# Order of transposes and copies, and softmax times v over two query blocks, in a streaming encoder step

## The chip, the cores and the metric

The kernel runs on one core of a Trainium2 chip. The metric is the device time of one execution in microseconds (us). TensorE (PE in the profile) multiplies and transposes, VectorE (DVE) and ScalarE (ACT) work elementwise and read the accumulators in PSUM, GpSimd (POOL) and SyncE (SP) mostly start transfers. Each engine works through its own instructions in order and waits for the others on semaphores.

## The reference

One layer of an encoder is applied to 1024 prompt rows and 64 sample rows (1088 in all) of width 1024. What the change touches is the attention; the layer reads:

```
h = rms_norm(x)
glu_a, glu_b, q, k, v, gates = split(h @ w_in)
u = glu_a * sigmoid(glu_b)
c = silu(layer_norm(causal_dwconv(u, width 31))) @ w_conv_out
for each of 16 heads (64 wide), each frame over its own 64-row chunk and the 8 chunks before:
    pr = softmax(q k^T / 8 + rel_bias)
    a = pr @ v
x = x + (sigmoid(gates_c) * c + sigmoid(gates_a) * (a @ w_att_out)) @ w_out
x = x + (gelu(causal_dwconv(up, width 3)) * gate) @ w_ffn_down        # up, gate from rms_norm(x) @ w_ffn_up
x = x + sigmoid(rms_norm(x) @ w_ple_gate) * (p @ w_ple_proj)
y = rms_norm(x)
```

Outputs are y, the new key and value caches and the convolution states, all in float32.

## The kernel before, in words

Activations stand with features on the 128 partitions and rows along the free dimension. A product of float32 operands is done as three products of their high and low parts (`mm3`, lines 154 to 166): a value is split by ACT, which copies the high part, and by DVE, which subtracts it (`split_into`, `w_split`).

The first part of the kernel, up to about 1010 us, makes the input projection in 40 + 16 jobs of 128 output columns (`order_1a`: gate `gb` and value `ga` of the GLU, `q`, `k`, `v`, the branch gates `s`). A job has three groups of rows (384, 384, 320 columns), a group 24 products of the type of line 159 to 161. Everything else is put between them by `tick`, which is called twice per group: in the middle (after 12 products) and at its end, after `evac` has emptied the accumulator. Ticks alternate; in this part those in the middle are "even" and those at the end "odd".

A head pair (two heads, 128 features) has nine query blocks, `p` = 0 to 7 of 128 prompt rows with 1, 2, 3, 4, 5, 5, 5, 5 key blocks of 128, and `p` = 8 with the 64 sample rows. A block goes through five steps:

- `step_S`, in an even tick: scores on PE into the PSUM tile `s_ps` (line 485), then on DVE the bias is added and a row minimum taken (line 491), which writes `s` to SBUF.
- `step_E`, same tick: exp on ACT (line 501).
- `step_R`, in the next odd tick: reciprocal on DVE (575), and ACT scales `s` (526).
- `step_T`, in the odd tick after that: PE transposes `s` block by block into the PSUM tile `t_ps` (511), and ACT copies that to `pt` (514; 516 and 519 for the sample block). `t_ps` holds both heads, one in each half, and shares its only buffer (tag `st`) with `s_ps`.
- `step_PV`, in the next even tick, behind the scores of a later block: softmax times v on PE into `o_ps` (536), its split into `aT` by ACT and DVE (170, 171), and a store to `a_d` by POOL (540), which is read back in the next part of the kernel.

Between those, `bg_tick` takes background work from a list: the 31 taps of the depthwise convolution on DVE (329), and from about 800 us the layer norm behind it (388 to 421), whose affine (409) and tanh (415) run on ACT. `tick` sums up the PE time that it reckons for a tick (`spent`), and 0.46 of it is what background work may cost. The order is thus fixed when the program is built; no scheduler moves it.

Of the kernel before, what the change touches and what calls it, by code (L numbers as in the profile page):

```python
# [9 lines left out]
F32 = mybir.dt.float32  # L10
F32R = mybir.dt.float32r
# [5 lines left out]
P = 128  # L17
# [58 lines left out]
def encoder_step(ctx: ExitStack, tc: tile.TileContext, I, O):  # L76
    nc = tc.nc
    dma_in = nc.sync.dma_start
    dma_st = nc.gpsimd.dma_start
# [17 lines left out]
    a_d = dram.tile([KT, P, 2, T], F32, name="a_d")  # L97
# [70 lines left out]
    def split_into(dst, c0, n, src, scale=1.0):  # L168

        nc.scalar.activation(out=dst[:, 0, c0:c0 + n], in_=src, func=AF.Copy, scale=scale)  # L170
        nc.vector.scalar_tensor_tensor(out=dst[:, 1, c0:c0 + n], in0=src, scalar=scale,
                                       in1=dst[:, 0, c0:c0 + n].bitcast(F32), op0=ALU.mult, op1=ALU.subtract)
# [47 lines left out]
    with tc.manual_schedule():  # L220
# [53 lines left out]
        at = att.enter_context(tc.tile_pool(name="att", bufs=1))  # L274
# [34 lines left out]
        def bg_tick(budget, most):  # L309
            debt[0] = min(debt[0] + budget, 2.5)  # L310
            while bg and debt[0] > 0 and most > 0:
                cost, fn = bg.pop(0)
                fn()
                debt[0] -= cost
                most -= 1
# [28 lines left out]
        st = {}  # L344
# [113 lines left out]
        cur = {}  # L458
        pipe = []
        stages = {"e": [], "t": [], "pv": []}  # L460
# [37 lines left out]
        def step_E(st):  # L498
            m, n = st["m"], st["n"]
            for s, sm in zip(st["s"], st["sm"]):  # L500
                nc.scalar.activation(out=s[0:m, 0:n], in_=s[0:m, 0:n], func=AF.Exp, scale=-1.0, bias=sm[0:m, 0:1],  # L501
                                     accum_out=sm[0:m, 1:2])

        def step_T(st):
            m, n = st["m"], st["n"]
            ps = ps_st[0].tile([P, 2, 1024], F32, tag="st", name="t_ps")
            st["pt"] = []
            for h, s in enumerate(st["s"]):
                for b in range(st["nb"]):
                    w = min(P, n - b * P)  # L510
                    nc.tensor.transpose(ps[0:w, h, b * P:b * P + m], s[0:m, b * P:b * P + w], ident[0:m, 0:m])  # L511
                pt = at.tile([P, 640], F32, tag="pt", name="pt", bufs=2)
                if m == P:
                    nc.scalar.activation(out=pt[:, 0:n], in_=ps[:, h, 0:n], func=AF.Copy)  # L514
                else:
                    nc.scalar.activation(out=pt[:, 0:512].rearrange("p (b q) -> p b q", q=P)[:, :, 0:m],
                                         in_=ps[:, h, 0:512].rearrange("p (b q) -> p b q", q=P)[:, :, 0:m],
                                         func=AF.Copy)
                    nc.scalar.activation(out=pt[0:64, 512:512 + m], in_=ps[0:64, h, 512:512 + m], func=AF.Copy)
                st["pt"].append(pt)  # L520

        def step_R(st):

            m, n = st["m"], st["n"]
            for s, sm in zip(st["s"], st["sm"]):
                nc.scalar.activation(out=s[0:m, 0:n], in_=s[0:m, 0:n], func=AF.Copy, scale=sm[0:m, 2:3])

        def step_PV(st):

            c, m, n, nb = cur[st["i"]], st["m"], st["n"], st["nb"]  # L530
            o_ps = ps_o.tile([P, 512], F32, tag="o", name="o_ps")
            for b in range(nb):
                w = min(P, n - b * P)
                for h in range(2):
                    a = 64 * h
                    nc.tensor.matmul(o_ps[a:a + 64, 0:m], lhsT=c["v"][0:w, st["vb"] + b, a:a + 64],  # L536
                                     rhs=st["pt"][h][0:w, b * P:b * P + m], start=(b == 0), stop=(b == nb - 1))
            aT = at.tile([P, 2, P], F32R, tag="aT", name="aT")
            split_into(aT, 0, m, o_ps[:, 0:m])
            dma_st(out=a_d[st["i"]][:, :, st["q0"]:st["q0"] + m], in_=aT[:, :, 0:m].bitcast(F32))  # L540

        pe_bg = []

        def tick(base=1.95):


            spent = base
            odd = turn[0]
            turn[0] = 1 - odd
            new = done = flip = None  # L550
            if not odd:
                if pipe:
                    new = pipe.pop(0)
                    spent += 1.1
                if stages["pv"]:
                    done = stages["pv"].pop(0)
                    spent += 0.218 * done["nb"] + 0.2
            elif stages["t"]:
                flip = stages["t"].pop(0)
                spent += 0.214 * flip["nb"]  # L560
            if new is not None:
                step_S(new)
            bg_tick(RATIO * spent, 1)
            if done is not None:
                step_PV(done)
            if new is not None:
                step_E(new)
                stages["e"].append(new)
            if flip is not None:
                step_T(flip)  # L570
                stages["pv"].append(flip)
            if odd:
                for st in stages["e"]:
                    for sm in st["sm"]:
                        nc.vector.reciprocal(out=sm[0:st["m"], 2:3], in_=sm[0:st["m"], 1:2])
                    step_R(st)
                    stages["t"].append(st)
                stages["e"].clear()
            if pe_bg:
                if pe_bg[0][0] <= 0:  # L580
                    pe_bg.pop(0)[1]()
                else:
                    pe_bg[0][0] -= 1
            bg_tick(0.0, 9)
# [58 lines left out]
        def job_group(kind, i, g, hl):  # L643
            c0, n = GR[g]
            ps_full = pjp.tile([P, 512], F32, tag="pj", name="pj")
            mm3(ps_full[:, 0:n], hl, hT, c0, n, hook=tick)
            evac(kind, i, g, ps_full[:, 0:n])
            tick()

        def evac(kind, i, g, ps):  # L650
                c0, n = GR[g]
# [27 lines left out]
                elif kind == "q":  # L679
                    c = cur[i]  # L680
                    split_into(c["Q"], c0, n, ps, scale=-0.125)
                elif kind == "k":
                    c = cur[i]
# [1 line left out]
                    for o, w, d in segs(c0, n, 0, SEQ + PAST):  # L685
                        nc.scalar.activation(out=kt[:, 0, d:d + w], in_=ps[:, o:o + w], func=AF.Copy)
                    if g == 1:
                        c["kst"] = at.tile([P, 640], F32, tag="pt", name="kst", bufs=2)
                        nc.scalar.activation(out=c["kst"][:, 0:256], in_=ps[:, 128:384], func=AF.Copy)
                    elif g == 2:  # L690
                        nc.scalar.activation(out=c["kst"][:, 256:576], in_=ps, func=AF.Copy)
                        dma_st(out=O["k_new"][i], in_=c["kst"][:, 0:576])
# [3 lines left out]
                elif kind == "v":  # L696
                    c = cur[i]
# [174 lines left out]
        while pipe or stages["t"] or stages["pv"] or pe_bg or bg:  # L872
            tick()
# [597 lines left out]
        for ci, ch in enumerate(chunks[:-1]):  # L1471
# [23 lines left out]
            for f in range(f0, KT):  # L1495
                hl = w_use()
                for g, (c0, n) in enumerate(GR):
# [5 lines left out]
                    if g == 1 and f in nxt:  # L1503
                        pool, tag = (bp, "pb") if ci == 1 else (ap_, "pair")
# [145 lines left out]
```

## Time and profile before

| what | value |
|---|---|
| median of 3 runs | 2203.5 us (2201.48 to 2205.72) |
| profiled execution | 2199.4 us, its span 2197.3 us |
| PE busy | 2094.6 us, 95% of the span |
| DVE, ACT, POOL busy | 1320.1, 829.8, 224.2 us |
| mean granted clock of TensorE | 0.99 of full speed |

The profile is of one execution. "Busy" is the time in which an engine worked; "idle before" is the time for which it stood still ahead of an instruction, with the engine and line whose end released it. PE's matmuls overlap, so a run of them is best measured from start to start. PEld is TensorE's weight load, which overlaps PE.

### The profile page before, as it was taken

The page shows a single profiled execution, that of the slowest core. Times are in us where ns is not written, and L with a number is a line of the kernel's source. Part 1 is how long each engine was busy: PE and PEld are TensorE (multiplying, and loading weights), DVE is VectorE, ACT ScalarE, POOL GpSimd, SP SyncE. Part 2 cuts the span into 40 slices and gives each one's busy share as a digit, 9 for nine tenths or more (in the row PEclk, how much of TensorE's full clock was granted, in tenths as well). Part 3 has the DMA queues.
Part 4 walks back from the last instruction along what each step waited for, and adds up shares of the span by engine and source line. Part 5 has one row for each costly group of instructions (what it writes and reads, how often), then busy time and mean ns, then how long its engine had stood idle before and what let it go on. Part 6 is the DMA issues. An engine that isn't in the chain of part 4 may idle for free.

```text
span 2197.3 us, 35659 instructions
## 1 busy us (share of the span) xinstructions
PE 2094.6 (95%) x14696; PEld 2012.2 (92%) x14696; DVE 1320.1 (60%) x2246; ACT 829.8 (38%) x1583; POOL 224.2 (10%) x453
## 2 busy tenths in 40 slices
PE   8989899999999998979999999999999999999997
PEld 6979798988888887869999999999999999999997
DVE  6676676676766645343235457777777763345644
ACT  5352635344545446473012334333333331113421
POOL 4000101101010111111000000000000020000400
PEclk9999999999999999999999999999999999999999
DMA  3312121212121221113533341212212144331011
GB/s 135 106 35 90 64 86 49 94 50 87 51 90 47 92 76 67 58 54 134 200 128 133 118 138 40 89 69 80 89 60 89 71 161 165 123 121 45 11 58 53
DMA packets 64706, 192.54 MB, mean 88 GB/s; under 512 B 8368, under 2 KB 22976, under 8 KB 63200
## 3 DMA queue, kind: packets, MB, share of 16 engines
q1 hardware_dynamic: 43072, 104.00, 13.8%
q0 software_dynamic: 21328, 85.71, 10.9%
q8 instruction: 115, 1.88, 0.4%
q10 hardware_dynamic: 144, 0.56, 0.1%
q14 instruction: 47, 0.39, 0.1%
HBM read 146.18 MB, written 54.01 MB: 91 GB/s over the span
## 4 chain that ended last, share of the span: by engine, by line
PE 82%; ACT 7%; DVE 5%; issue 4%; DMA 1%; POOL 0%; SPq 0%; POOLq 0%; ACTq 0%; DVEq 0%
PE pj L159 15%; PE pj L161 14%; PE pj L160 14%; PE pj L1159 7%; PE pj L1160 7%; PE pj L1158 7%; PE pj L1461 3%; PE pj L1460 3%; PE pj L1459 3%; PE o_ps L536 2%; PE t_ps L511 2%; PE s_ps L485 2%; ACT pt L514 2%; ACT s L501 1%; DVE c L329 1%
## 5 line engine op out<-in xcount | busy, mean ns | idle before, releaser
L159 PE MATMUL pj<-hT,whl 128*128 128x384 f32 (+1 forms) x1296 | 444.3, 343 | 0.7 <-ACT sg L677 0.7
L160 PE MATMUL pj<-hT,whl 128*128 128x384 f32 (+1 forms) x1296 | 427.0, 329 | 0.0
L161 PE MATMUL pj<-hT,whl 128*128 128x384 f32 (+1 forms) x1296 | 426.7, 329 | 0.3 <-DVE whl L135 0.3
L329 DVE SCALAR_TENSOR_TENSOR c<-u,cc,c 128x1118 f32<-128x1118 f32 x240 | 330.7, 1378 | 2.4
L159 PEld LDWEIGHTS pj<-hT,whl 128*128 128x128 f32 x1296 | 246.2, 190 | 14.2 <-issue 10.9
L161 PEld LDWEIGHTS pj<-hT,whl 128*128 128x128 f32 x1296 | 245.8, 190 | 0.6 <-DVE whl L135 0.6
L160 PEld LDWEIGHTS pj<-hT,whl 128*128 128x128 f32 x1296 | 245.9, 190 | 0.0
L1158 PE MATMUL pj<-mp,wq 128*128 128x272 f32 x704 | 204.2, 290 | 5.0 <-ACT ug L1234 2.7
L1160 PE MATMUL pj<-mp,wq 128*128 128x272 f32 x704 | 204.6, 291 | 0.0
L1159 PE MATMUL pj<-mp,wq 128*128 128x272 f32 x704 | 204.4, 290 | 0.0
L135 DVE TENSOR_TENSOR whl<-raw,whl 128x1024 fp32r<-128x1024 f32 (+3 forms) x100 | 115.8, 1159 | 137.0 <-ACT whl L134 136.9
L134 ACT ACTIVATE whl<-raw 128x1024 fp32r<-128x1024 f32 (+3 forms) x100 | 100.1, 1001 | 221.5 <-PE pj L1461 133.7
L491 DVE CUSTOM_DVE_ANT_0 s<-s_ps,bias 128x640 f32<-128x640 f32 (+3 forms) x144 | 90.4, 664 | 145.2 <-PE s_ps L485 145.0
L1135 ACT ACTIVATE wq<-raw 128x512 fp32r<-128x512 f32 x144 | 84.3, 625 | 191.0 <-DVE raw L1144 135.6
L511 PE MATMUL t_ps<-ident,s 128*128 128x128 f32 (+2 forms) x560 | 86.7, 277 | 71.9 <-ACT pt L514 66.8
L511 PEld LDWEIGHTS t_ps<-ident,s 128*128 128x128 f32 (+2 forms) x560 | 61.9, 141 | 92.0 <-ACT pt L514 82.5
L1460 PE MATMUL pj<-gp,whl 128*128 128x384 f32 (+1 forms) x432 | 141.3, 327 | 0.3 <-DVE gp L1369 0.3
L1461 PE MATMUL pj<-gp,whl 128*128 128x384 f32 (+1 forms) x432 | 141.3, 327 | 0.2 <-DVE whl L135 0.2
L1459 PE MATMUL pj<-gp,whl 128*128 128x384 f32 (+1 forms) x432 | 141.0, 326 | 0.0
L1158 PEld LDWEIGHTS pj<-mp,wq 128*128 128x128 f32 x704 | 134.1, 191 | 5.4 <-ACT ug L1234 2.9
L1159 PE MATMUL pj<-bq,wq 128*128 128x272 f32 x480 | 138.6, 289 | 0.0
L1160 PE MATMUL pj<-bq,wq 128*128 128x272 f32 x480 | 138.3, 288 | 0.0
(255 smaller groups left out, 4716.9 us busy)
## 6 DMA issues: line engine op xcount, KB each, us to landing
raw<-in_w_in SPq DMA_DIRECT2D x56, 512.0 KB, 3.5
raw<-in_w_ffn_up SPq DMA_DIRECT2D x44, 512.0 KB, 4.5
q_d<-ug POOLq DMA_DIRECT2D x22, 544.0 KB, 3.0
gp<-q_d POOLq DMA_DIRECT2D x22, 544.0 KB, 7.3
tg<-s_d POOLq DMA_DIRECT2D x16, 544.0 KB, 3.9
aP<-a_d POOLq DMA_DIRECT2D x8, 1088.0 KB, 6.0
a_d<-aT POOLq DMA_DIRECT2D x64, 128.0 KB, 2.2
f_d<-e_d POOLq DMA_DIRECT2D x16, 383.5 KB, 4.9
```

The costliest lines, as they stand in the source:

```text
L135: nc.vector.tensor_tensor(out=hl[:, 1, 0:k, :], in0=raw[:, 0:k, :], in1=hl[:, 0, 0:k, :].bitcast(F32), op=ALU.subtract)
L159: nc.tensor.matmul(ps, lhsT=wsel(hl, 0, k), rhs=r[:, 0, c0:c0 + n], start=(k == 0), stop=False)
L160: nc.tensor.matmul(ps, lhsT=wsel(hl, 0, k), rhs=r[:, 1, c0:c0 + n], start=False, stop=False)
L161: nc.tensor.matmul(ps, lhsT=wsel(hl, 1, k), rhs=r[:, 0, c0:c0 + n], start=False, stop=(k == K - 1))
L329: nc.vector.scalar_tensor_tensor(out=c_t[f], in0=u_t[f][:, j:j + CCOL], scalar=pc("conv_dw", f * CW + j), in1=c_t[f], op0=ALU.mult, op1=AL ...
L511: nc.tensor.transpose(ps[0:w, h, b * P:b * P + m], s[0:m, b * P:b * P + w], ident[0:m, 0:m])
L1158: nc.tensor.matmul(ps, lhsT=q[:, 0, kt, :], rhs=h, start=start and kt == 0, stop=False)
L1159: nc.tensor.matmul(ps, lhsT=q[:, 0, kt, :], rhs=l, start=False, stop=False)
L1160: nc.tensor.matmul(ps, lhsT=q[:, 1, kt, :], rhs=h, start=False, stop=stop and kt == 3)
L1459: nc.tensor.matmul(ps, lhsT=hl[:, 0, k, :], rhs=h, start=k == 0, stop=False)
L1460: nc.tensor.matmul(ps, lhsT=hl[:, 0, k, :], rhs=l, start=False, stop=False)
L1461: nc.tensor.matmul(ps, lhsT=hl[:, 1, k, :], rhs=h, start=False, stop=k == K - 1)
```

## The change

In `step_T` the transposes of both heads are issued first, then both copies. `step_PV` takes a list of blocks: `tick` waits until two have been transposed (or the sample block stands first), computes both into one `o_ps` side by side, and splits and stores them in one step of 256 columns. `pt` gets four buffers in place of two (also for `kst`, which shares its tag), and `aT` becomes twice as wide.

```diff
             for h, s in enumerate(st["s"]):
                 for b in range(st["nb"]):
                     w = min(P, n - b * P)
                     nc.tensor.transpose(ps[0:w, h, b * P:b * P + m], s[0:m, b * P:b * P + w], ident[0:m, 0:m])
-                pt = at.tile([P, 640], F32, tag="pt", name="pt", bufs=2)
+            for h in range(2):
+                pt = at.tile([P, 640], F32, tag="pt", name="pt", bufs=4)
                 if m == P:
                     nc.scalar.activation(out=pt[:, 0:n], in_=ps[:, h, 0:n], func=AF.Copy)
...
-        def step_PV(st):
-
-            c, m, n, nb = cur[st["i"]], st["m"], st["n"], st["nb"]
+        def step_PV(sts):
+
+
             o_ps = ps_o.tile([P, 512], F32, tag="o", name="o_ps")
-            for b in range(nb):
-                w = min(P, n - b * P)
-                for h in range(2):
-                    a = 64 * h
-                    nc.tensor.matmul(o_ps[a:a + 64, 0:m], lhsT=c["v"][0:w, st["vb"] + b, a:a + 64],
-                                     rhs=st["pt"][h][0:w, b * P:b * P + m], start=(b == 0), stop=(b == nb - 1))
-            aT = at.tile([P, 2, P], F32R, tag="aT", name="aT")
-            split_into(aT, 0, m, o_ps[:, 0:m])
-            dma_st(out=a_d[st["i"]][:, :, st["q0"]:st["q0"] + m], in_=aT[:, :, 0:m].bitcast(F32))
+            n = 0
+            for st in sts:
+                c, m, nb = cur[st["i"]], st["m"], st["nb"]
+                for b in range(nb):
+                    w = min(P, st["n"] - b * P)
+                    for h in range(2):
+                        a = 64 * h
+                        nc.tensor.matmul(o_ps[a:a + 64, n:n + m], lhsT=c["v"][0:w, st["vb"] + b, a:a + 64],
+                                         rhs=st["pt"][h][0:w, b * P:b * P + m], start=(b == 0), stop=(b == nb - 1))
+                n += m
+            aT = at.tile([P, 2, 2 * P], F32R, tag="aT", name="aT")
+            split_into(aT, 0, n, o_ps[:, 0:n])
+            q0 = sts[0]["q0"]
+            dma_st(out=a_d[sts[0]["i"]][:, :, q0:q0 + n], in_=aT[:, :, 0:n].bitcast(F32))
...
-                if stages["pv"]:
-                    done = stages["pv"].pop(0)
-                    spent += 0.218 * done["nb"] + 0.2
+                if len(stages["pv"]) == 2 or (stages["pv"] and stages["pv"][0]["p"] == 8):
+                    done = list(stages["pv"])
+                    stages["pv"].clear()
+                    spent += sum(0.218 * st["nb"] for st in done) + 0.2
...
-                        c["kst"] = at.tile([P, 640], F32, tag="pt", name="kst", bufs=2)
+                        c["kst"] = at.tile([P, 640], F32, tag="pt", name="kst", bufs=4)
```

ACT's order at an odd tick, before, with what each row waits for: an evacuation (`u<-pj`), the two copies `pt`, the two scalings `s`. Ahead of them stand a weight split (`whl<-raw`), the split of `o_ps` and the exps of the even tick.

```order
L134 ACTIVATE whl<-raw 128x1024 [waits DMAHW7_49]
L170 ACTIVATE aT<-o_ps 128x128 [waits DMASW5_49,PE_49]
L501 ACTIVATE s,sm<-s,sm 128x640 [waits DVE_49] x2
L662 ACTIVATE u<-pj 128x384 [waits PE_49]
L514 ACTIVATE pt<-t_ps 128x640 [waits PE_49,Activation_49] x2
L526 ACTIVATE s<-s,sm 128x640 [waits DVE_49] x2
```

The same place now (line numbers behind the change are a few higher):

```order
L134 ACTIVATE whl<-raw 128x1024 [waits DMAHW7_49]
L170 ACTIVATE aT<-o_ps 128x256 [waits DMASW1_49,PE_49]
L501 ACTIVATE s,sm<-s,sm 128x640 [waits DVE_49] x2
L669 ACTIVATE u<-pj 128x384 [waits PE_49]
L515 ACTIVATE pt<-t_ps 128x640 [waits PE_49]
L515 ACTIVATE pt<-t_ps 128x640
L527 ACTIVATE s<-s,sm 128x640 [waits DVE_49] x2
```

Before, each copy waits for PE; now only the first does, and it waits for the transposes of both heads. The split of `o_ps` has 256 columns.

PE's order at the even tick of the sample block's scores (`p` = 8), before: the last of 12 products, the scores, softmax times v of one block (two heads with five key blocks), and the products go on.

```order
L161 MATMUL pj<-hT,whl 128x384
...
L485 MATMUL s_ps<-K,Q 64x288 x12
L536 MATMUL o_ps<-pt,v 64x128 x10
L159 MATMUL pj<-hT,whl 128x320
L160 MATMUL pj<-hT,whl 128x320
L161 MATMUL pj<-hT,whl 128x320
```

PE now, from the scores of the block ahead of it (`p` = 7) on:

```order
L485 MATMUL s_ps<-K,Q 128x320 x12
L540 MATMUL o_ps<-pt,v 64x128 x20
...
L511 MATMUL t_ps<-ident,s 128x128 x10
...
L485 MATMUL s_ps<-K,Q 64x288 x12
L159 MATMUL pj<-hT,whl 128x320
L160 MATMUL pj<-hT,whl 128x320
L161 MATMUL pj<-hT,whl 128x320
```

Softmax times v of two blocks now stands behind the scores of `p` = 7; behind those of `p` = 8 there is none, and twelve products follow at once, then the transposes.

## Rows read from the trace of the kernel before

**Rows 1.** The page's first part: the span, and the first line of the busy times.

```profile
span 2197.3 us, 35659 instructions
...
PE 2094.6 (95%) x14696; PEld 2012.2 (92%) x14696; DVE 1320.1 (60%) x2246; ACT 829.8 (38%) x1583; POOL 224.2 (10%) x453
```

**Rows 2.** Busy time by stretch (start:end, its length, each engine's busy us with its instructions, then the granted clock, the share of the DMA engines and GB/s).

```profile
90.00:780.00 690.00, 643.06 (x4641) 591.16 (x4640) 471.18 (x729) 317.15 (x701) 72.42 (x147) 1.00 0.21 69
...
900.00:1010.00 110.00, 92.35 (x651) 82.99 (x650) 42.00 (x86) 69.61 (x129) 13.89 (x23) 0.94 0.17 59
```

**Rows 3.** The transposes' group on PE, from the page (busy us, mean ns of one, idle us before it and what ended it), and the waits of PE by stretch (us in total, times, longest): 90 to 780 us (two rows), 780 to 900, 900 to 1010. In the last two there is one more row each, of 0.6 us, for line 519.

```profile
L511 PE MATMUL t_ps<-ident,s 128*128 128x128 f32 (+2 forms) x560 | 86.7, 277 | 71.9 <-ACT pt L514 66.8
...
PE t_ps L511 <- ACT pt L514: 43.1, 48, 4.4
PE t_ps L511 <- ACT pt L519: 3.8, 6, 0.6
...
PE t_ps L511 <- ACT pt L514: 8.5, 8, 2.2
...
PE t_ps L511 <- ACT pt L514: 15.2, 8, 2.6
```

**Rows 4.** The timeline of one step of the third head pair, without the products (start, us, engine, line; in brackets the idle time before it and what ended it): scores (a run of softmax times v follows them), DVE's two reductions, then head 0's transposes and copy, head 1's transposes and copy, and the next scores.

```profile
376.09 1.14 PE L485 MATMUL s_ps<-K,Q 64*128 64x320 f32 x12
...
377.27 0.82 DVE L491 CUSTOM_DVE_ANT_0 s<-s_ps,bias 128x640 f32<-128x640 f32 x1 [3.81 <-PE s_ps L485]
...
378.02 0.82 DVE L491 CUSTOM_DVE_ANT_0 s<-s_ps,bias 128x640 f32<-128x640 f32 x1
...
380.60 0.71 PE L511 MATMUL t_ps<-ident,s 128*128 128x128 f32 x5
381.41 0.70 ACT L514 ACTIVATE pt<-t_ps 128x640 f32<-128x640 f32 x1 [0.99 <-PE t_ps L511]
382.16 0.77 PE L511 MATMUL t_ps<-ident,s 128*128 128x128 f32 x5 [0.85 <-ACT pt L514]
383.03 0.70 ACT L514 ACTIVATE pt<-t_ps 128x640 f32<-128x640 f32 x1 [0.92 <-PE t_ps L511]
384.96 1.15 PE L485 MATMUL s_ps<-K,Q 64*128 64x320 f32 x12
```

**Rows 5.** The same view at 140 us, first head pair: an evacuation of `gb` on ACT, head 1's transposes, and the next scores.

```profile
140.63 0.49 ACT L662 ACTIVATE u<-pj 128x384 f32<-128x384 f32 x1 [4.15 <-DVE c L329]
...
141.77 1.33 PE L511 MATMUL t_ps<-ident,s 128*128 128x128 f32 x5 [4.40 <-ACT pt L514]
...
145.82 1.15 PE L485 MATMUL s_ps<-K,Q 64*128 64x320 f32 x12
```

**Rows 6.** The same view: scores and the next transposes in a tick without softmax times v (the second block), head 1's transposes of the third block, and the fifth block (three key blocks in its softmax times v), with DVE ahead of its reduction.

```profile
340.14 0.62 PE L485 MATMUL s_ps<-K,Q 64*128 64x256 f32 x6
342.89 0.27 PE L511 MATMUL t_ps<-ident,s 128*128 128x128 f32 x1
...
357.41 0.55 PE L511 MATMUL t_ps<-ident,s 128*128 128x128 f32 x3 [0.69 <-ACT pt L514]
...
359.99 1.14 PE L485 MATMUL s_ps<-K,Q 64*128 64x320 f32 x12
...
360.74 1.23 DVE L135 TENSOR_TENSOR whl<-raw,whl 128x1024 fp32r<-128x1024 f32 x1 [2.97 <-ACT whl L134]
361.89 0.82 DVE L491 CUSTOM_DVE_ANT_0 s<-s_ps,bias 128x640 f32<-128x640 f32 x1
...
364.08 0.60 PE L511 MATMUL t_ps<-ident,s 128*128 128x128 f32 x4
```

**Rows 7.** The split of `o_ps` into `aT`, by line (duration in ns: least, median, most; first and last start; forms): the least is of 64 columns, the median of 128.

```profile
L170 ACT ACTIVATE aT<-o_ps x72: 223/277/280, 103.3 to 1000.3; 128x128 fp32r<-128x128 f32 x64, 128x64 fp32r<-128x64 f32 x8
...
L171 DVE SCALAR_TENSOR_TENSOR aT<-o_ps,aT x72: 216/284/292, 105.2 to 1000.6; 128x128 fp32r<-128x128 f32 x64, 128x64 fp32r<-128x64 f32 x8
```

**Rows 8.** The timeline in the last head pair: a weight split, the scores of one block, its exps' two parts, an evacuation, the affine, a copy, head 1's transposes, a scaling, the tanh, and the scores three blocks on.

```profile
939.11 1.05 ACT L134 ACTIVATE whl<-raw 128x1024 fp32r<-128x1024 f32 x1
...
949.56 1.15 PE L485 MATMUL s_ps<-K,Q 64*128 64x320 f32 x12
...
951.95 0.82 ACT L501 ACTIVATE s<-s,sm 128x640 f32<-128x640 f32 x1
...
952.67 0.19 ACT L501 ACTIVATION_READ_ACCUMULATOR s<-s,sm 128x1 f32 x1
...
953.72 0.53 ACT L677 ACTIVATE sg<-pj,cc 128x320 f32<-128x320 f32 x1
954.15 1.31 ACT L409 ACTIVATE c<-c,cc 128x1118 f32<-128x1118 f32 x1
955.36 0.69 ACT L514 ACTIVATE pt<-t_ps 128x640 f32<-128x640 f32 x1
956.10 0.77 PE L511 MATMUL t_ps<-ident,s 128*128 128x128 f32 x5 [1.87 <-ACT pt L514]
957.57 0.82 ACT L526 ACTIVATE s<-s,sm 128x640 f32<-128x640 f32 x1
959.00 1.12 ACT L415 ACTIVATE lsq<-c 128x1118 f32<-128x1118 f32 x1
...
980.10 1.01 PE L485 MATMUL s_ps<-K,Q 64*64 64x288 f32 x12
```

## The prediction

> **What bounds the kernel now.** I read the page's busy line first: PE works 2094.6 of 2197.3 us [rows 1], so the time can only fall where PE stands still. The windows by stretch say where: PE stands still for 47 of the 690 us from 90 to 780, and for 18 of the 110 from 900 to 1010 [rows 2]. That is the attention stretch (780 to 900 lies in it too), and there the waits name one cause. Of the second head's transposes the page says 71.9 us of idle, ended by a copy `pt` on ACT (line 514 or 519) [rows 3]; by stretch that is 43.1 + 3.8 = 46.9, then 8.5 + 0.6 = 9.1, then 15.2 + 0.6 = 15.8 us, together 71.8. Hardly anything else idles PE there.
>
> The timeline of one step shows the wait whole [rows 4]. Head 0's five transposes start at 380.60, ACT copies them from 381.41 to 382.11, head 1's start at 382.16, the copy of those ends at 383.73, and the next scores start at 384.96. Both heads are halves of one tile `t_ps`, and the second half waits until the first has been copied.
>
> **The transposes.** In the new order both heads' transposes stand together, and only the first copy behind them waits for PE. So the wait inside a step is gone by construction. Its worth: head 1's transposes start 1.56 us behind head 0's; without the wait it would be about 0.67 (382.16 to 384.96 is 2.80, less the 2.13 that twelve products take with a change of work, derived below). That is 0.89 us, close to the 0.85 of idle in the row, and I use the idle totals.
>
> What is late next? Both copies now start when all transposes have ended, so the last ends about 0.70 (one copy) later after the last transpose than before. The scores that reuse the PSUM buffer stood 384.96 - 383.73 = 1.23 us behind it [rows 4]; 0.53 is left, and some 0.18 where the twelve products between have 320 columns (2.13 x 320/384 = 1.78, 0.35 less). Softmax times v, behind the scores, has 1.15 us more. Cost nothing, while ACT is on time.
>
> ACT is not on time in one place of the conv part: at 140.63 the evacuation of `gb` ends a wait of 4.15 us for DVE's taps, the copies queue behind it, and PE waits 4.40 [rows 5]. There both copies would end at 140.63 + 0.49 + 2 x 0.70 = 142.52, and the scores start then, not at 145.82: 3.3 saved of 4.4, so 1.1 stays.
>
> This is a rule against the change as well: the Trainium skill ("PSUM — Partial Sum Buffer", Engine vs sequencer instructions) says that ScalarE's and VectorE's queues are strictly first in, first out. By it a delay ahead of the copies isn't removed but handed on to the next scores. The row at 140.63 agrees; what it would do everywhere is the first rival below.
>
> **Softmax times v in pairs.** The instructions for it are the same in number; 32 runs of 72 go away (four of nine steps per head pair, eight pairs). What a run costs apart from its products comes from the distance between the end of the scores and the next transposes: 342.89 - 340.76 = 2.13 with no run between, 364.08 - 361.13 = 2.95 with three key blocks, 380.60 - 377.23 = 3.37 with five [rows 4, 6]. Two blocks cost 0.42, so a block 0.21; 2.95 - 2.13 - 3 x 0.21 leaves 0.19 per run. 32 x 0.19 = 6.0 us gained. It could be nothing (if the change of work is paid anyway) or twice as much; I take the rows' value.
>
> The split of 256 columns in place of two of 128: ACT 277 ns at 128 and 223 at 64 columns, DVE 284 and 216 [rows 7]. By these two widths 256 would take about 277 + 2 x 54 = 385 and 284 + 2 x 68 = 420 ns; an estimate, 0.17 and 0.15 us less than twice 128 each. POOL issues 32 stores fewer, of twice the bytes; nothing reads `a_d` before the attention is over. All beside PE: nothing. The planner books 32 x 0.2 x 0.46 = 2.9 us less for background work, some two taps over eight head pairs; nothing.
>
> What the pairs take away is cover. In an even tick without softmax times v, the next transposes come 2.13 us after the scores and need DVE to have read them: two reductions of 0.75 + 0.82 = 1.57 us and the hand-over, 0.05 as in 382.11 to 382.16 [rows 4]. If DVE starts at once (0.04 at 377.27) there is room, 0.5 us. At the fifth block it doesn't: DVE is still subtracting the next weights, and starts 0.76 late, at 361.89 against 361.13 [rows 6]. This is one of the blocks that lose their cover, and its scores come 0.69 earlier, by what the transposes before them no longer wait (357.41 [rows 6]), so the lag grows to about 1.45: 1.45 + 1.57 + 0.05 - 2.13 = 0.94 of new wait, eight times 7.5 us. From below: nothing. From above: at each of the 32 ticks, and with one more weight subtraction in front of it (1.23 [rows 6]), 0.94 + 1.23 = 2.2, in all 69, which is the slower rival's ground. I take the one block whose row shows a lag.
>
> The exps of an even tick stand behind the split on ACT, so a pair delays them by one more run, 1.2 us. They feed a reciprocal and a scaling that the transposes need two ticks later; covered.
>
> **The last head pair.** From 900 us the layer norm's affine (1.31) and tanh (1.12) join ACT, and transposes wait some 1.9 us in place of 0.85 [rows 8]. One block asks of ACT: evacuation 0.53, affine 1.31, copies 2 x 0.69, scalings 2 x 0.77 (0.82 less the overlap), tanh 1.12, exps 2 x 1.01, half a pair's split 0.19, a third of a weight split 0.35: 8.4 us. The scores stand 30.54 us apart over three blocks (949.56 to 980.10), 10.2 each. So ACT, not PE, sets the floor there: 10.2 - 8.4 = 1.8 us a block can go, 12.3 over seven such blocks of the 14.5 they wait (15.8 less 1.3 in the first and last step). 12.3 + 1.3 - 0.9 (the fifth block) = 12.7 us. The granted clock of that stretch is 0.94, against 1.00 before [rows 2]; where ACT is the floor I book nothing for it.
>
> **The sum.** 90 to 780 us: 46.9 - 1.1 - 6 x 0.94 = 40.2. 780 to 900: 9.1 - 0.9 = 8.2. Last pair 12.7. Runs 6.0. Together 67.1 us. The profiled execution took 2199.4 us (its span 2197.3); it would take 2132.3. It stands 4.1 under the median of the runs, 2203.5, so the median becomes 2136.
>
> **Rivals.**
> First, ACT hands the wait on: in the conv part, too, the copies come late and the scores wait. For it: a block asks 6.0 us of ACT there (the sum above without affine and tanh), against a period that shrinks from 8.87 (376.09 to 384.96) to about 7.8, and the margin is only 0.18 to 0.53. Against: ACT is busy 317 of 690 us [rows 2], and the copy itself began promptly in the step shown. If half of the 46.9 and half of the 12.7 stay, the gain is 67.1 - 23.5 - 6.4 = 37.2: 2166.
>
> Second, more goes than I book: no new DVE wait (7.5) and the clock of the last stretch comes back (92.35 us of PE work x 0.06 = 5.5): 2203.5 - 80 = 2123.5 (67.1 + 7.5 + 5.5 = 80.1). The row's evidence is that the clock is 1.00 where the waits are 0.85 and 0.94, so in part at 1.2 instead of 2.4 GHz, where they are 1.9. The Trainium skill ("TensorE: Matmul & The Clock Gate", Why this matters for your kernels) warns of idle gaps between bursts of matmuls as what lowers the clock, which by itself would argue for this rival; no row here separates it from ACT's load.
>
> Third, slower: DVE takes the place of the wait. In the 32 ticks without softmax times v, the transposes come 2.13 us after the scores; each microsecond that DVE is late beyond 0.51 is a microsecond of PE. To lose the 67.1 and 4.4 more needs 71.5 / 32 = 2.23 us each, a lag of 2.74 at all of them. For it: DVE is busy 471 of 690 us and would be near 73%. Against: the lags in the rows are 0.04 and 0.76, and DVE had stood idle 3.81 us ahead of the reductions at 377.27 [rows 4]. At 2.4 us each it ends at 2203.5 - 67.1 + 77 = 2213.
>
> Fourth, it doesn't do what it says: head 1's transposes still wait for ACT in the new program. What they wait for must stand ahead of both copies on ACT, since the copies wait for these transposes; it can only be the scaling of `s`, two ticks old. Only the 6.0 of the runs would be left: 2197.5.
>
> **How the numbers follow.** Forecast 0.70 (own range 2122 to 2151: on one side the 7.5 gone and the 6.0 doubled, on the other the 7.5 tripled), first rival 0.17, second 0.08, third 0.03, fourth 0.02. About 0.2%, 4.4 us, is what a measurement can tell from no change. The first two rivals and the fourth are faster, though the fourth by little, so I give faster 0.95, same 0.02, slower 0.03. The range takes in most of the second and of the first rival: 2116 to 2168.
>
> **What would show it.** L511's idle ended by ACT's copies falls from 71.9 us to under 5; L511 gets a new idle ended by DVE's reductions (L491), about 7; L485 gets one ended by `pt`, a few us, in the layer norm's stretch and once near 140. PE's busy time in 90 to 780 stays near 643 while that stretch ends some 40 us earlier. In the last stretch ACT is busy nearly all the time. I am wrong if L485's or L511's new idle is over 25 us, or if PE's busy time itself grows.

## The result, and the profile after

The changed kernel takes 2118.7 us (median, 2116.42 to 2120.73) against 2204.6 of the kernel before (the three executions behind the 2203.5 above and a fourth, 2207.3): ratio 0.961, 95% interval 0.9594 to 0.9627, so 3.9% faster. All times here are such medians; one execution of another kernel, 5167 us against 2110 to 2115 for the four beside it, is left out of its median. The profiled execution has a span of 2119.0 us, 78.3 less than before; by medians the gain is 85.9, since the execution profiled before was 5.2 under its runs' median and the one after 2.0 above its own. Much of that goes with TensorE's mean granted clock. The two profiled executions had 0.990 and 0.991. But the kernel before had 0.986 to 0.990 in the 31 executions made beside the experiments below, 0.989 in the middle one, and the changed kernel 0.991 to 0.995 in eight, mostly 0.992 to 0.994. Among the executions of one of these kernels 0.001 of clock goes with 1.2 to 1.5 us, so some 5 of the 85.9 us came with the clock, an estimate from these figures.

The page after, its first part, answers to [rows 1]:

```profile
span 2119.0 us, 35395 instructions
...
PE 2075.2 (98%) x14696; PEld 2011.5 (95%) x14696; DVE 1318.2 (62%) x2214; ACT 819.3 (39%) x1551; POOL 204.3 (10%) x421
```

PE executes as many matmuls as before, 14696, but its busy time has fallen as well, by 19.4 us. The forecast had said that it would stay. The groups of three lines on PE, and of the split of `o_ps`, from the view by line (busy us, mean ns of one, idle before and what ended it); the first row answers to [rows 3]:

```profile
L511 PE MATMUL t_ps<-ident,s 128*128 128x128 f32 (+2 forms) x560 | 69.8, 267 | 9.9 <-DVE sm L491 9.9
L485 PE MATMUL s_ps<-K,Q 64*128 64x320 f32 (+4 forms) x672 | 69.4, 331 | 5.9 <-ACT pt L515 5.9
L540 PE MATMUL o_ps<-pt,v 128*64 128x128 f32 (+2 forms) x1120 | 67.9, 271 | 0.0
...
L170 ACT ACTIVATE aT<-o_ps 128x256 fp32r<-128x256 f32 (+1 forms) x40 | 14.2, 354 | 53.0 <-PE o_ps L540 53.0
L171 DVE SCALAR_TENSOR_TENSOR aT<-o_ps,aT 128x256 fp32r<-128x256 f32 (+1 forms) x40 | 15.2, 380 | 22.8 <-ACT aT L170 22.8
```

The 71.9 us that the transposes waited for ACT are gone. Two new waits stand in their place, 9.9 for DVE and 5.9 of the scores for the copies. The waits of PE, from 80 to 1010 us, by what ended them (us in total, times, longest):

```profile
PE t_ps L511 <- DVE sm L491: 9.9, 8, 2.5
PE s_ps L485 <- ACT pt L515: 5.9, 4, 3.5
```

The timeline of the third head pair, two blocks, without most products, answers to [rows 4]:

```profile
357.60 1.15 PE L485 MATMUL s_ps<-K,Q 64*128 64x320 f32 x12
...
360.90 1.25 PE L511 MATMUL t_ps<-ident,s 128*128 128x128 f32 x10
361.91 0.42 PE L159 MATMUL pj<-hT,whl 128*128 128x384 f32 x1
...
364.18 1.14 PE L485 MATMUL s_ps<-K,Q 64*128 64x320 f32 x12
365.25 2.40 PE L540 MATMUL o_ps<-pt,v 128*64 128x128 f32 x40
367.58 0.44 PE L159 MATMUL pj<-hT,whl 128*128 128x384 f32 x1
...
372.72 1.01 PE L485 MATMUL s_ps<-K,Q 64*64 64x288 f32 x12
```

Ten transposes stand in one run, and the next product starts 361.91 - 360.90 = 1.01 us after the first of them. From scores to scores it is now 6.58 us without softmax times v and 8.54 with two blocks of it, 15.12 together; before, one of these distances was 8.87 [rows 4].

Where the gain was made shows in the starts of the scores: the first of the first, seventh and eighth head pairs, and the first split of the stage behind the attention, stood at 91.03, 790.29, 908.33 and 1007.49 us, and now at 91.81, 741.37, 851.20 and 930.1. So the first six head pairs became 49.7 us shorter, the seventh 8.2, the last 20.3: 78.2, all of it.

Busy time by stretch, with the granted clock (columns as in [rows 2], to which this answers):

```profile
90.00:740.00 650.00, 639.17 (x4702) 601.80 (x4701) 475.83 (x709) 313.77 (x683) 57.15 (x123) 1.00 0.22 74
740.00:840.00 100.00, 98.34 (x733) 92.13 (x732) 47.65 (x93) 57.70 (x116) 11.86 (x22) 0.97 0.21 73
840.00:930.00 90.00, 85.42 (x662) 78.62 (x661) 40.45 (x80) 67.11 (x123) 10.55 (x19) 1.00 0.20 69
```

In the last stretch PE stands still for 4.6 of 90 us, where it was 18 of 110, and its clock is the full 2.4 GHz (1.00) in place of 0.94.

### The profile page after: what moved, and what is told of

Read it like the earlier page. It is cut to its first block, busy times and chain, and to the rows that moved or that the text cites. A ratio compares the mean times of both kernels' runs of the same rounds, so it can differ in the third digit from the quotient of the medians.

```text
span 2119.0 us, 35395 instructions
## 1 busy us (share of the span) xinstructions
PE 2075.2 (98%) x14696; PEld 2011.5 (95%) x14696; DVE 1318.2 (62%) x2214; ACT 819.3 (39%) x1551; POOL 204.3 (10%) x421
## 4 chain that ended last, share of the span: by engine, by line
PE 88%; DVE 6%; ACT 3%; issue 2%; DMA 1%; POOL 0%; POOLq 0%; SPq 0%; DVEq 0%; ACTq 0%
PE pj L159 16%; PE pj L161 15%; PE pj L160 15%; PE pj L1166 7%; PE pj L1167 7%; PE pj L1165 7%; PE pj L1468 3%; PE pj L1467 3%; PE pj L1466 3%; PE o_ps L540 3%; PE s_ps L485 3%; PE t_ps L511 2%; DVE c L329 1%; DVE s L491 1%; DVE acc L1012 1%
## 5 line engine op out<-in xcount | busy, mean ns | idle before, releaser
L159 PEld LDWEIGHTS pj<-hT,whl 128*128 128x128 f32 x1296 | 244.3, 188 | 15.5 <-issue 12.3
L1165 PEld LDWEIGHTS pj<-mp,wq 128*128 128x128 f32 x704 | 134.1, 190 | 5.4 <-ACT ug L1241 2.9
L1166 PE MATMUL pj<-bq,wq 128*128 128x272 f32 x480 | 138.5, 288 | 0.0
L1167 PE MATMUL pj<-bq,wq 128*128 128x272 f32 x480 | 138.3, 288 | 0.0
L1165 PE MATMUL pj<-bq,wq 128*128 128x272 f32 x480 | 138.0, 288 | 0.0
L1166 PEld LDWEIGHTS pj<-mp,wq 128*128 128x128 f32 x704 | 134.0, 190 | 0.0
```

What stands on the lines that cost most here:

```text
L159: nc.tensor.matmul(ps, lhsT=wsel(hl, 0, k), rhs=r[:, 0, c0:c0 + n], start=(k == 0), stop=False)
L1165: nc.tensor.matmul(ps, lhsT=q[:, 0, kt, :], rhs=h, start=start and kt == 0, stop=False)
L1166: nc.tensor.matmul(ps, lhsT=q[:, 0, kt, :], rhs=l, start=False, stop=False)
L1167: nc.tensor.matmul(ps, lhsT=q[:, 1, kt, :], rhs=h, start=False, stop=stop and kt == 3)
```

## The experiments

Two accounts of the result were open. By the first, the transposes alone make the gain and the pairs add their 6 us less the new DVE waits; by the second, ACT's order or the clock makes part of it. Each experiment takes one piece away or adds one.

**Each part alone.** The transposes alone, from the kernel before:

```diff
+            for h in range(2):
                 pt = at.tile([P, 640], F32, tag="pt", name="pt", bufs=2)
```

> Only the first part of the change: the transposes of both heads ahead of their copies; softmax times v stays one block at a time. Theory: a run of transposes has a price of its own of some 0.19 us for the change to and from the products, as a run of softmax times v has, so that each of the 72 steps gains its wait and one run: 71.8 + 72 x 0.19 = 85.5 us, less some 6 us that the scores wait for late copies and nothing for DVE, as every even tick keeps its cover: about 79 us under the kernel before, 2125. PE's busy time of the transposes falls from 86.7 to about 70 us. Rival: the gain beyond the waits comes from the pairing; then this kernel gains no more than about 66 us (2138), and the transposes' busy time stays near 80. The granted clock of the last head pair's stretch rises from 0.94 to nearly 1.00 if the waits lowered it.

And the pairs alone: the changed kernel, with each copy again right behind its head's transposes.

```diff
-            for h in range(2):
                 pt = at.tile([P, 640], F32, tag="pt", name="pt", bufs=4)
```

> Only the second part of the change: softmax times v in pairs, with each head's transposes followed by its copy as before. Theory: 32 runs less at 0.19 us are 6 us, and the fifth block of each head pair waits for DVE by up to 0.25 us (lag 0.76, no stall of the step before taken away), 2 us in all: 4 us under the kernel before, about 2200.5, hardly more than can be measured. The waits for the copies stay near 72 us and the clock of the last pair's stretch near 0.94. Rival: the pairing brings the 20 us that the forecast of the whole lacks, 2185.

The transposes alone took 2116.8 us, ratio 0.961 (0.9597 to 0.9623); the pairs alone 2209.2, ratio 1.0025 (1.0015 to 1.0036). The first is 8 us better than its expectation, the second 9 worse: it is slower than the kernel before by some 6 us. The groups on PE of the first:

```profile
L537 PE MATMUL o_ps<-pt,v 128*64 128x128 f32 (+2 forms) x1120 | 75.1, 274 | 0.2 <-ACT pt L515 0.2
L511 PE MATMUL t_ps<-ident,s 128*128 128x128 f32 (+2 forms) x560 | 69.7, 266 | 2.9 <-DVE sm L491 2.9
L485 PE MATMUL s_ps<-K,Q 64*128 64x320 f32 (+4 forms) x672 | 69.5, 331 | 5.6 <-ACT pt L515 5.6
```

and of the second:

```profile
L511 PE MATMUL t_ps<-ident,s 128*128 128x128 f32 (+2 forms) x560 | 85.9, 275 | 79.3 <-ACT pt L514 70.6 <-ACT pt L519 6.6 <-DVE sm L491 2.1
...
L539 PE MATMUL o_ps<-pt,v 128*64 128x128 f32 (+2 forms) x1120 | 67.0, 270 | 0.0
```

The whole gain is the transposes'. The same 560 instructions are busy 85.9 us where they wait in the middle, 69.7 where they don't. The pairs take some 7 us off softmax times v in either kernel (75.1 to 67.9, 74.1 to 67.0), and lose it: with the transposes together to DVE (9.9 in place of 2.9), alone to longer waits for the copies (77.2 in place of 71.9) and for DVE (2.1). That this kernel is even slower than the one before was not traced further.

**The DVE wait.** The fifth block's reductions stand behind a weight split on DVE. In the changed kernel that split was put behind the middle tick of the second group:

```diff
-                if g == 0:
-                    w_ahead(1)
+        def tick_split():
+            tick()
+            w_ahead(1)
...
-            mm3(ps_full[:, 0:n], hl, hT, c0, n, hook=tick)
+            mm3(ps_full[:, 0:n], hl, hT, c0, n, hook=tick_split if g == 1 else tick)
```

> The changed kernel, with the split of the next weights issued behind the scores of the second group's middle tick instead of behind the first group. Theory: in the changed kernel the fifth block of every head pair waits for DVE, which is still subtracting those weights (9.9 us in 8 waits); with the subtraction behind the reductions those waits go nearly all, and the time falls by 8 to 10 us, to about 2110. Rival: DVE is late there for its whole load, not for this one subtraction; then the waits move to other blocks and the time stays within 3 us of 2119.

It took 2111.3 us, ratio 0.9585 (0.9572 to 0.9598), 7.5 under the changed kernel. Its waits:

```profile
PE s_ps L485 <- ACT pt L515: 8.0, 8, 3.5
...
PE t_ps L511 <- DVE sm L491: 0.4, 1, 0.4
```

All but 0.4 of the DVE wait went; 2.1 came back at the scores, 1.8 of it in one place of the last head pair (2.36 at 874.68 us in place of 0.58), where the copies on ACT now stand behind the later split (871.12). A second time, in another batch:

> The kernel with pairs and the later weight split, again, on the same chip as the next. Theory: 32 runs less at 0.07 us, 2 us, and as many waits: 2 us under the next kernel. Rival: 5 us under it (0.16 a run).

2112.5 us, ratio 0.9584 (0.9571 to 0.9597). The kernel that it was expected to beat by 2 or 5 us, under "What the pairs are worth", took 2112.2: neither came.

**ACT in the last head pair.** From the kernel with the later split, the layer norm's affine moved from ACT to DVE:

```diff
-                return lambda: nc.scalar.activation(out=c_t[f], in_=c_t[f], func=AF.Identity,
-                                                    scale=pc("conv_ln_g", f), bias=pc("conv_ln_b", f))
+                return lambda: nc.vector.tensor_scalar(out=c_t[f], in0=c_t[f], scalar1=pc("conv_ln_g", f),
+                                                       scalar2=pc("conv_ln_b", f), op0=ALU.mult, op1=ALU.add)
```

> The kernel with the later weight split, and in it the affine step of the layer norm on DVE instead of ACT (one instruction of scale and shift, eight in all; 1.31 us each on ACT, about 0.9 on DVE). Theory: ACT is no floor in the last head pair any more, since PE's only waits for ACT there are 3.6 us; so at most those go, and the time falls by 0 to 3.5 us, to 2108 to 2111. Rival, as the forecast had it: ACT sets the length of a block there; then some 1.3 us go in each of the last six or seven blocks, 8 us, 2103.

> The kernel with pairs, the later weight split and the affine step on DVE, again, beside the one without that last step. Theory: 1.6 us less waiting for ACT, so 1 to 3 us under it, about 2109. Rival: the first time's 2.6 us were chance, and both are the same within 1 us.

They took 2108.7 (ratio 0.9578, 0.9562 to 0.9594) and 2108.9 us (0.9568, 0.9555 to 0.9581), 2.6 and 3.7 under the kernel they start from, whose intervals (0.9572 to 0.9598 and 0.9571 to 0.9597) overlap these; so it is a gain of a few us at most. From 860 to 900 us, with the affine on ACT:

```profile
860.00:880.00 20.00, 17.64 (x149) 15.97 (x148) 13.24 (x27) 18.98 (x33) 2.46 (x4) 1.00 0.18 63
880.00:900.00 20.00, 19.41 (x166) 17.73 (x164) 11.48 (x20) 19.06 (x31) 2.33 (x4) 1.00 0.24 79
```

and with it on DVE:

```profile
860.00:880.00 20.00, 18.84 (x150) 17.45 (x149) 16.32 (x29) 17.05 (x32) 3.04 (x5) 1.00 0.24 82
880.00:900.00 20.00, 19.41 (x169) 18.06 (x169) 14.71 (x26) 16.38 (x30) 1.82 (x4) 1.00 0.18 60
```

In the second stretch ACT went from 19.06 of 20 us to 16.38, and PE's busy time is 19.41 in both: there PE is itself full, and a full ACT didn't hold it up. In the first PE gained 1.2 us, at the one place where the scores waited 2.36 us for the copies and now wait 1.17. The distances between the scores show the same: from the fifth scores of the last head pair to the ninth they were 8.44, 7.91, 6.65 and 9.20 us, and are 7.24, 7.90, 6.58 and 9.21. So ACT held up one block, not each.

**What a run of transposes costs.** From the kernel with the transposes alone, head 0's were issued three products ahead of head 1's, so that there are 72 runs more and no wait for a copy between them; then one product ahead. (`flip_head` issues one head's transposes.)

```diff
+        def early_T():
+            if turn[0] and stages["t"]:
+                flip_head(stages["t"][0], 0)
...
-            mm3(ps_full[:, 0:n], hl, hT, c0, n, hook=tick)
+            mm3(ps_full[:, 0:n], hl, hT, c0, n, hook={3: tick, 6: early_T})
```

> The transposes ahead of their copies and softmax times v one block at a time, and head 0's transposes stand three products before the end of the group, so that the two heads' transposes are again two runs, with no wait for a copy between them. Theory: a second run costs 72 x 0.19 = 14 us more than the kernel with the transposes together and softmax times v single: about 2139, and PE's busy time of the transposes is back near 85. Rival: a run has no price of its own and only the wait counted: the same time as that kernel.

```diff
+            if late is not None and k == K - 1:
+                late()
...
+            mm3(ps_full[:, 0:n], hl, hT, c0, n, hook=tick, late=early_T)
```

> As the kernel whose transposes stand apart, but with only the last product of the group between head 0's and head 1's transposes, so that they start 0.17 instead of 0.5 us early and the waits for DVE stay near those of the kernel with the transposes together (2.9 us, at most 5). Theory now: a run of transposes costs only some 0.07 us more than its instructions, and what the forecast missed is the tail of head 0's transposes, 0.24 us each, which the wait laid bare and the profile counts as busy: 72 x 0.07 = 5 us and some 2 of waits over the kernel with softmax times v single, about 2124. Rival: a run costs 0.19 us, 14 us and 2 of waits: 2133.

The first took 2132.3 us (ratio 0.968, 0.9667 to 0.9693), 15.5 over the transposes in one run, as expected, but not for the reason given. Its transposes' group, its waits and a place in its timeline:

```profile
L510 PE MATMUL t_ps<-ident,s 128*128 128x128 f32 (+2 forms) x560 | 82.0, 267 | 13.5 <-DVE sm L491 13.5
...
PE t_ps L510 <- DVE sm L491: 13.5, 21, 1.3
```

```profile
372.02 0.34 PE L161 MATMUL pj<-hT,whl 128*128 128x384 f32 x1
372.20 0.71 PE L510 MATMUL t_ps<-ident,s 128*128 128x128 f32 x5
372.66 0.39 PE L159 MATMUL pj<-hT,whl 128*128 128x320 f32 x1
```

10.6 of the 15.5 are waits for DVE, which the earlier issue brought on (13.5 in place of 2.9). The rest, 4.9, is 0.07 per run, or less, since a wait can cost more than its idle time (see the first step below). The second kernel, with waits for DVE of 6.0, took 2124.8 us (0.965, 0.9636 to 0.9663), as expected and 8.0 over, of which 3.1 is DVE: again about 5 for 72 runs. The row at 372.20 shows another thing: five transposes keep PE for 0.46 us, though their busy time is 0.71. So the busy time of the transposes rose by 12.3 (69.7 to 82.0), near the 85 expected, while the runs cost 5: the tail of a run counts as busy, whether the next work waits for it or not.

**What the pairs are worth.** The transposes alone with the later split, so that the DVE wait is gone from both sides, twice:

> Transposes ahead of their copies, softmax times v one block at a time, and the later weight split. Theory: the pairing is worth 32 runs at about 0.16 us, 5 us, once its wait for DVE is gone; this kernel then stands some 5 us over the one with pairs and the later split (2111), at about 2116, and has hardly a wait for DVE. Rival: the later split alone is what made that kernel faster, and the pairing is worth nothing: 2111 to 2112.

> The kernel with softmax times v single and the later weight split, again: the one against which the two before it are read; about 2113.

2113.3 and 2112.2 us, ratios 0.9598 and 0.9582, against 2111.3 and 2112.5 us, 0.9585 and 0.9584, with the pairs: these don't tell the two apart. The rows of the second, one block of softmax times v:

```profile
360.28 1.31 PE L537 MATMUL o_ps<-pt,v 128*64 128x128 f32 x20
361.52 0.44 PE L159 MATMUL pj<-hT,whl 128*128 128x384 f32 x1
```

One block takes 1.24 us up to the next product, two in one run 2.33 (367.58 - 365.25, in the timeline after): a pair saves 2 x 1.24 - 2.33 = 0.15. Over 32 that is 4.8. Some 2 of it go back, since the scores wait 8.0 us for the copies with the pairs against 5.0 (and softmax times v 1.3) without.

The other way round, softmax times v was cut in two runs, three products apart, 64 runs more (`end_PV` issues the second):

```diff
-            for b in range(nb):
+            pv_blocks(st, c, o_ps, range(0, (nb + 1) // 2))
+            late_pv.append((st, c, o_ps))
...
+            pv_blocks(st, c, o_ps, range((st["nb"] + 1) // 2, st["nb"]))
...
+            mm3(ps_full[:, 0:n], hl, hT, c0, n, hook={3: tick_split if g == 1 else tick, 4: end_PV})
```

> As the kernel with softmax times v single and the later weight split, but each block's softmax times v in two runs, three products apart: half of its key blocks behind the scores, the rest and the split of o_ps three products later. That is 64 runs more (the first block of each head pair has one key block and stays whole), with no wait of PE added that the trace of that kernel shows. Theory: a run of softmax times v costs some 0.07 us beside its products, as one of transposes does, not the 0.19 of the forecast; 64 x 0.07 = 4.5 us over the kernel with single runs. Rival: 0.17 to 0.19 a run, 11 to 12 us over it.

2131.4 us (0.9669, 0.9656 to 0.9682), 19.1 over the kernel with one run in the same batch: both expectations missed it. A place in its timeline, all of PE:

```profile
360.40 0.34 PE L160 MATMUL pj<-hT,whl 128*128 128x384 f32 x1
360.57 0.34 PE L161 MATMUL pj<-hT,whl 128*128 128x384 f32 x1
360.84 0.66 PE L544 MATMUL o_ps<-pt,v 128*64 128x128 f32 x8
361.43 0.44 PE L159 MATMUL pj<-hT,whl 128*128 128x384 f32 x1
361.71 0.34 PE L160 MATMUL pj<-hT,whl 128*128 128x384 f32 x1
```

Two products follow each other after 0.17 to 0.18; into the run it takes 0.27, and behind it the second product comes after 0.28, 0.1 more each. The waits of PE for `pt` are 2.5 us fewer than with one run, so a run between products costs about 0.34 ((19.1 + 2.5) / 64), one behind scores 0.15. Part of the difference is in the starts: behind scores the 0.28 after the run (361.52 to 361.80 with one run) is there without a run as well (130.07 to 130.35 in the changed kernel). Nothing was run on it.

**The changed kernel once more**, beside the second batch:

> The changed kernel once more, beside these. Theory: 2118.7 within 2 us, so that its differences to the kernel with only the transposes moved (2116.8) and to the one with the later split (2111.3) are read on the same footing; L511 waits 10 us for DVE and L485 6 us for the copies again.

2119.5 us, ratio 0.9625 (0.9611 to 0.9639), with the same waits, 9.9 and 5.9 us. The best kernel here, with pairs, later split and affine on DVE, took 2108.7 in the same batch, 10.8 less.

## Why the prediction was right, and where its sizes were off

The sign, the cause and the place were as forecast, and the time lies inside the range. The forecast, 2136, is 17 us too high; the result is 3 us outside the likeliest case's own range, and 2.7 inside an end that was set for the second rival. So it is the width of the range that took it in, and not the sum. By steps:

**"Its worth: 0.89 us ... I use the idle totals."** This step failed in size. The idle ahead of a waiting transpose starts only when head 0's transposes count as ended, 0.71 us after they start [rows 4]. But work that follows at once starts 0.46 after them (the row at 372.20). The 0.25 between counts as busy time of PE, and goes with the wait. From head 0's transposes to the first product it was 2.09 us before (380.60 [rows 4] to 382.69, the next row of that timeline, below), and is 1.01 now, so a step gains 1.08 and not 0.85.

```profile
382.69 0.43 PE L159 MATMUL pj<-hT,whl 128*128 128x384 f32 x1
```

My "0.67" for head 1's transposes without the wait was in truth 0.53 (382.16 to 382.69): it was to be seen ahead. Over 72 steps, some of them with fewer transposes, L511's busy time fell from 86.7 [rows 3] to 69.8. The account of the profiles closes with it: of 71.8 us of wait the forecast had taken 61.1 as gained, and 71.9 - 9.9 - 5.9 = 56.1 were; softmax times v is 6.2 us shorter by its busy time (74.1 to 67.9) for the 6.0 booked; with the 16.9 that is 79.2, against the 78.3 measured. So this one term makes up the gain that had not been booked, and 5 us more, which new waits took. The groups' busy times hold the clock as well: in the last head pair (below) part of the gain is the clock's.

**"At the fifth block ... 0.94 of new wait, eight times."** Seven such waits came, in the fifth block of each head pair but the seventh, and an eighth of 0.18 in a later block (263.61); together 9.9 us for the 7.5 booked. Four took 1.04, as at 118.32. Three are larger: 1.23 at 234.68, 1.75 at 346.92 and 2.55 at 881.39. DVE and PE in the second of these:

```profile
341.72 1.14 PE L485 MATMUL s_ps<-K,Q 64*128 64x320 f32 x12
...
344.06 1.23 DVE L135 TENSOR_TENSOR whl<-raw,whl 128x1024 fp32r<-128x1024 f32 x1 [2.29 <-ACT whl L134]
345.20 0.82 DVE L491 CUSTOM_DVE_ANT_0 s<-s_ps,bias 128x640 f32<-128x640 f32 x1
...
346.92 1.06 PE L511 MATMUL t_ps<-ident,s 128*128 128x128 f32 x8 [1.75 <-DVE sm L491]
```

DVE had itself waited 2.29 us for ACT's half of the weight split. Moving the split (the third experiment above) took all seven waits away, which shows the cause; the 0.4 that is left is in the other block.

**"32 x 0.19 = 6.0 us" for the pairs.** A pair saves 0.15, so 4.8, and with the 7.0 of DVE waits that are there only with the pairs the second half of the change is worth nothing. The forecast had both terms, 6.0 and 7.5, and had put the second down to the lost cover, but didn't say that it cancels the first.

**"So 1.1 stays", at 140 us.** There 3.50 stays:

```profile
137.41 0.49 ACT L669 ACTIVATE u<-pj 128x384 f32<-128x384 f32 x1 [4.62 <-DVE c L329]
137.79 1.29 ACT L515 ACTIVATE pt<-t_ps 128x640 f32<-128x640 f32 x2
...
139.14 1.70 PE L485 MATMUL s_ps<-K,Q 64*128 64x320 f32 x10 [3.50 <-ACT pt L515]
```

From the evacuation to the scores it is 1.73 us; the step had said 0.49 + 1.40 = 1.89, so that part is right. But the evacuation is on DVE's time: it starts 8.42 us behind the scores before it (128.99), as before (8.48, 132.15 to 140.63). Softmax times v, which PE did in that time before, has moved to another tick, and its 1.24 us (133.22 to 134.46 before) have turned into wait. Another 1.2 is the clock's: from head 1's transposes to the scores it was 4.05 us there (141.77 to 145.82 [rows 5]), with a granted clock of 0.91 from 140 to 160 us, and 2.80 in [rows 4]; now PE does that work at full clock ahead of the scores, and waits longer. The Trainium skill ("PSUM — Partial Sum Buffer", Engine vs sequencer instructions) says that ScalarE's queue is strictly first in, first out; the copies behind an evacuation that waited 4.62 us agree.

**The last head pair: 12.7 booked and its share of the runs, 0.8; 20.3 measured.** "So ACT, not PE, sets the floor there" was wrong: with 1.3 us less for ACT in a block only one block became shorter (the affine on DVE, above). From 880 us on, by stretch:

```profile
880.00:900.00 20.00, 18.03 (x148) 16.64 (x150) 12.58 (x25) 19.19 (x33) 2.32 (x4) 1.00 0.20 68
900.00:920.00 20.00, 19.79 (x192) 18.16 (x189) 11.11 (x20) 19.27 (x30) 2.31 (x4) 1.00 0.17 60
```

"ACT is busy nearly all the time" came true here, 38.5 of 40 us, though not over the whole stretch (67.11 of 90 us from 840 to 930); and yet PE stood still for only 2.2, of which 1.4 is the DVE wait that ends at 881.39. From the second scores to the ninth, the seven blocks for which 12.3 was booked, it was 65.01 us (915.09 to 980.10) and is 50.21 (857.94 to 908.15): 14.8 gained. From the ninth scores to the end of the pair it was 27.39 and is 21.95: 5.4 gained, for 1.3 booked in the first and last step. From the fifth scores to the ninth a block came to 8.2 us ((908.15 - 875.40) / 4), close to the step's 8.4, but by luck: 3.3 of these 32.75 us were waits, 2.55 of them for DVE, and the rest PE's own work. Besides, the clock came back, from 0.94 to 1.00, which I had booked at nothing and the second rival at 5.5. In this stretch it goes with the waits: with the pairs alone, where they stay, it shows 0.95:

```profile
900.00:1010.00 110.00, 95.03 (x688) 86.74 (x687) 41.25 (x83) 67.54 (x123) 12.50 (x20) 0.95 0.16 57
```

and with the transposes alone, in its last stretch, 1.00, though ACT's load is no smaller there (69.52 of 90 us):

```profile
840.00:930.00 90.00, 84.85 (x644) 76.86 (x645) 44.39 (x89) 69.52 (x131) 13.89 (x23) 1.00 0.23 76
```

The Trainium skill ("TensorE: Matmul & The Clock Gate", Why this matters for your kernels) warns that gaps between bursts of matmuls lower the clock; the trace agrees in this stretch. Waits alone don't settle the clock elsewhere. Two stretches of the kernel before with much the same busy time of PE, and one of the changed kernel in which PE never stands still:

```profile
840.00:860.00 20.00, 15.89 (x138) 13.94 (x136) 11.61 (x19) 15.01 (x26) 2.47 (x4) 1.00 0.31 104
920.00:940.00 20.00, 15.88 (x87) 13.92 (x86) 8.04 (x18) 13.68 (x26) 2.47 (x4) 0.83 0.13 42
...
760.00:780.00 20.00, 20.00 (x156) 18.51 (x153) 6.88 (x16) 13.42 (x28) 2.46 (x4) 0.91 0.18 60
```

Between the two profiled executions the clock gave next to nothing over the whole kernel, since 740 to 840 us now has 0.97; between the medians it is some 5 us (see the result). Why the stretch from 740 us fell wasn't tried.

**By stretch.** The first six pairs were booked at 40.2 and their share of the runs, 4.5, and gained 49.7; the seventh at 8.9 and gained 8.2; the last as above. 78.2 less 67.1 is 11.1. The other 6 us of the miss are the way from one execution to the median: I had added 4.1, and the execution after stands 2.0 above its median. By the clocks in the section on the result, much of that goes with the clock.

**The rivals.** The second (2123.5) came nearest, by the clock but not by the DVE waits, which came. The first, ACT handing the wait on, is at 5.9 us in four places, not 30. The third asked 2.4 us of DVE at 32 ticks; it is eight ticks at 1.2 on average. The fourth is out: no copy ends a wait of L511.

## What to carry to other kernels

The idle time that this profile shows ahead of a waiting matmul was a lower bound of what the wait cost: the tail of the work before it counts as busy. Take the distance from start to start with the wait and, elsewhere in the trace, without it; here that is 1.08 us in place of 0.85, 17 us of 79. An engine that is busy 96% of a stretch needn't be its floor: here some of ACT's work was taken away, and all blocks but one kept their length. And where a change has two parts, work out each alone: here one made all the gain, and the other paid for its 5 us with 7 of waiting.

## What was not expected of the hardware

Ten float32 transposes of 128x128 in one run keep PE 1.01 us, 0.1 each, though the mean of one is 267 ns. What a change of work on PE costs depends on its neighbours: 0.07 us for a run of transposes between products, 0.15 for a run of softmax times v behind scores, about 0.34 for one between products.
